# Retention in a hybrid decoder step: the output formed transposed with the values as weights, and the eight chunk states formed by one scan

## The chip, the core and the metric

The kernel is one launch on one of the eight cores of a Trainium2 chip. A core has five engines with separate instruction queues: TensorE (PE in the profile, its weight loads as PEld), VectorE (DVE), ScalarE (ACT), GpSimd (POOL) and SyncE (SP), which here issues most DMAs. Each engine runs its own queue in order; semaphores tie the queues together. TensorE reads SBUF and writes PSUM. The metric is the device time in microseconds of the launch, the median of several runs.

## The reference

The reference is one step of a decoder layer with two parallel branches, sparse attention and multi-scale retention, on a prompt of 1024 tokens and on 8 sequences of 4 new tokens. The change touches only the retention of the prompt, cut here to what is computed. There are 8 heads of 64 channels, and the prompt runs as 8 chunks of 128 tokens:

```python
def retention_chunk(state, q, k, v):
    ...
    scores = jnp.einsum('bihd,bjhd->bhij', q, k) * dmat
    out = jnp.einsum('bhij,bjhe->bihe', scores, v)
    q_decay = jnp.exp(lg[None, :] * (i[:, None] + 1.0))
    out = out + jnp.einsum('bihd,bhde->bihe', q, state) * q_decay[None, :, :, None]
    k_decay = jnp.exp(lg[None, :] * (C - 1.0 - i)[:, None])
    new_state = (jnp.exp(lg * C)[None, :, None, None] * state
                 + jnp.einsum('bjhd,bjhe->bhde', k * k_decay[None, :, :, None], v))
    return new_state, out
```

So each chunk's output is a product inside the chunk (scores times values) plus the queries times the state left by the chunks before it, and the state is a recurrence over the chunks: old state times one constant per head, plus this chunk's keys times values. The last state is an output of the layer. After it come a norm over each head's 64 channels, a gain and a gate.

## The kernel before

The program is written as one long Python function and its instructions are put into each engine's order by a scheduler that works with its own estimate of time; inside a group made by `together` the order is fixed. The chip then runs each engine's queue strictly in that order.

The stages, with the times of the profiled run: loads and norm (to about 90 us), a long stretch of projections of the input (to about 820 us) into which other work is woven, the prompt's attention (to 1030 us), and the output projection. A projection (`project`, L356 to L367) computes 128 output columns: three pieces of 352 tokens, each of 24 matrix products (L208, L209, L210: 8 steps of high and low parts), into one of two PSUM buffers `pj`. A buffer is free for the piece after next when ACT, and for some projections DVE as well, has read it. The weights of the next projection are loaded by SP (L188), and split by ACT (L194) and DVE or POOL (L195).

Two things are woven into the projections from about 160 us to 560 us:

- Retention, one `pair` of heads at a time (L428 to L567), four pairs one after the other. Each pair projects keys, queries, values and a gate (L458 to L479), turns keys and values into token rows (`kd`, `vtok`), and then does the retention. After a pair follow the projection of attention queries (`split_rows`, whose pieces are read by L391 on ACT and L392 on DVE, and the last by L396 too) and two of gates (L573).
- The selection of the top 256 keys for each query (`pick_all`, L793 to L807): 31 rounds of a bisection, in each of which DVE counts five blocks (L727), ACT counts two (L734), and DVE joins them into the next candidate (L743, L741, L803, L805). It ends with `finish` (L771 to L783), a fixed sequence of DVE operations on the seven blocks. DVE is nearly full while this runs.

The retention of a pair, where the change lies, has these steps:

- L484: for each of the 8 chunks and both heads, keys times values, into the PSUM tile `pk` (chunk by chunk, 64 columns each). The two heads of a pair occupy partitions 0 to 63 and 64 to 127.
- L486 to L488: a copy of chunk 0 and seven dependent DVE operations form the eight states `S`, chunk after chunk. The last one goes out by DMA (L489).
- L495 to L500: scores of keys and queries in two halves of four chunks, each multiplied by the decay mask on DVE into a tile `tmp` (`sT`).
- L507: queries times state, for chunks 7 to 1 and both heads. The stationary operand is the queries' 64 x 128 block of one head, the moving one the 64 columns of `S`. Result: tokens on partitions.
- L510: scores times values, stationary the 128 x 128 score block, moving the 64 columns of values, added to the same PSUM tile `po`.
- L512: ACT copies `po` into `O`, tokens on partitions.
- L516 to L539: the same for the 8 sample sequences: L524 and L529 to L532 on TensorE, L535 forms their state update `pn`, L538 adds it on DVE.
- L544 to L567: the norm over `O`, which begins on DVE with L544, then transposes (L563) back to channels on partitions, gain and gate, and a DMA out.

PSUM in this stage holds two buffers each of `pj`, `pl` (two banks) and `pt` (one bank); `pk`, `pn` and the transposes take turns in `pt`.

Of the kernel before, what the change touches and what calls it, by code (L numbers as in the profile page):

```python
# [8 lines left out]
F32 = mybir.dt.float32  # L9
# [4 lines left out]
OP = mybir.AluOpType  # L14
# [32 lines left out]
C_HM = C_SB8 + 16  # L47
C_ALL = C_HM + 32

R_G, R_GS, R_MB, R_ALL = 0, 4, 8, 16  # L50

M_D, M_S, M_ALL = 0, 256, 320


def shape_constants():
    f = np.float32
    p = np.arange(128)
    c = np.zeros((128, C_ALL), f)
    c[:, C_ID:C_ID + 128] = np.eye(128, dtype=f)
    c[:, C_CAUS:C_CAUS + 128] = np.where(p[None, :] > p[:, None], f(BIGNEG), f(0))  # L60
    b = np.arange(8)
    t = np.arange(32)
    c[:, C_MSK:C_MSK + 256] = (t[None, :] // 4 == b[:, None]).astype(f).reshape(1, 256)
    c[:, C_SEL:C_SEL + 32] = (p[:, None] % 32 == t[None, :]).astype(f)
    c[:32, C_MN:C_MN + 32] = np.where((t[None, :] // 4 == t[:, None] // 4) & (t[None, :] % 4 <= t[:, None] % 4),
                                      f(0), f(BIGNEG))
    c[0, C_BSEL:C_BSEL + 128] = 1.0
    for i in range(32):
        c[1 + i // 4, C_BSEL + 128 + i] = 1.0
    c[:, C_MH:C_MH + 8] = ((p[:, None] // 4) % 8 == b[None, :]).astype(f)  # L70
    c[:, C_SB8:C_SB8 + 16] = ((p[:, None] // 32 == t[None, :16] // 4) & (p[:, None] % 4 == t[None, :16] % 4)).astype(f)
    for q in range(4):
        c[:, C_HM + 8 * q:C_HM + 8 * q + 8] = (p[:, None] // 64 + 2 * q == b[None, :]).astype(f)
    r = np.zeros((128, R_ALL), f)
    m = np.zeros((4, 128, M_ALL), f)

    rot = np.zeros((4, 2, 128, 2 * TT), f)
    inv = (f(10000.0) ** (-np.arange(32, dtype=f) / f(32))).astype(f)
    pos = np.concatenate([np.arange(T), PAST + np.arange(NS) % NI]).astype(f)
    ang = (pos[:, None] * inv[None, :]).astype(f).T  # L80
    cos, sin = np.tile(np.cos(ang), (2, 1)), np.concatenate([-np.sin(ang), np.sin(ang)])
    step = np.concatenate([np.arange(T) % 128, np.arange(NS) % NI]).astype(f)
    size = np.concatenate([np.full(T, 128), np.full(NS, NI)]).astype(f)
    lg = np.log1p(-np.exp2(-5.0 - np.arange(8, dtype=f))).astype(f)
    df = (p[None, :] - p[:, None]).astype(f)
    ds = (t[None, :] - t[:, None]).astype(f)
    ok = (t[None, :] // 4 == t[:, None] // 4) & (ds >= 0)
    for h in range(8):
        q, i = divmod(h, 2)
        rows = slice(64 * i, 64 * i + 64)  # L90
        m[q, :, M_D + 128 * i:M_D + 128 * i + 128] = np.where(df >= 0, np.exp(lg[h] * f(-128.0)), 0)
        m[q, :32, M_S + 32 * i:M_S + 32 * i + 32] = np.where(ok, np.exp(lg[h] * f(-4.0)), 0)
        for a, decay in enumerate((np.exp(lg[h] * (size - f(1.0) - step)) * f(0.125), np.exp(lg[h] * (step + f(1.0))))):
            rot[q, a, rows, :TT] = cos * decay[None, :]
            rot[q, a, rows, TT:] = sin * decay[None, :]
        r[rows, R_G + q] = np.exp(lg[h] * f(128.0))
        r[rows, R_GS + q] = np.exp(lg[h] * f(4.0))
    r[:32, R_MB:R_MB + 8] = (t[:, None] // 4 == b[None, :]).astype(f)
    return c, r, m, rot
# [20 lines left out]
def _hybrid_step(ctx, tc, A, outs, dbg):  # L120
    nc = tc.nc
# [17 lines left out]
    def pl():  # L139
        return ps.tile([128, 1024], F32, name="pl", bufs=2)  # L140

    def pt():
        return ps.tile([128, 512], F32, name="pt", bufs=2)
# [3 lines left out]
    ident = C[:, C_ID:C_ID + 128]  # L147
# [83 lines left out]
    with ExitStack() as s0:  # L231
# [8 lines left out]
        rows = sp.tile([48, 128], F32, name="rows")  # L240
# [144 lines left out]
    def split_rows(pool, f0, p, dst, new, x=None):  # L385

        hl = [pool.tile([128, TT], F32R, name="raw", bufs=2) for _ in "hl"]

        def use(c, y):
            sl = slice(c * CH, c * CH + CH)  # L390
            nc.scalar.copy(hl[0][:, sl], y)  # L391
            nc.vector.tensor_sub(hl[1][:, sl], y, f32(hl[0][:, sl]))  # L392
            if x is not None:
                nc.scalar.copy(x[:, sl], y)  # L394
            if c == 2:
                nc.scalar.copy(new[:, p], y[:, CH - NS:])  # L396
        project(f0, use)
        for d, t in zip(dst, hl):
            nc.sync.dma_start(d[128 * p:128 * p + 128], f32(t[:, :T]))
# [3 lines left out]
    def retention(gp):  # L403
        with ExitStack() as s3:
            rp = s3.enter_context(tc.tile_pool(name="rp", bufs=1, reuse_waits="tile"))
            RC = rp.tile([128, R_ALL], F32, name="rc")
            nc.sync.dma_start(RC, A["rcs"])
            O = rp.tile([128, 9, 2, 64], F32, name="O")
            nc.gpsimd.memset(O[:, 8], 0.0)
            for p in range(4):  # L410
                pair(rp, RC, O, p)
                split_rows(gp, O_QA + 128 * p, p, QD, qs)
                gates(gp, (4 + 2 * p, 5 + 2 * p))

    def big(rp, name):
        return rp.tile([128, 9, 128], F32, name=name, bufs=2 if name == "tmp" else 1)
# [8 lines left out]
                nc.tensor.transpose(p[:n, t - 4 * g], src[:, t * 128:t * 128 + n], ident)  # L425
            use(4 * g, m, 128 if g < 2 else NS, p)

    def pair(rp, RC, O, p):  # L428
        flat = lambda t: t.rearrange("p t c -> p (t c)")[:, :TT]
        head = [slice(64 * i, 64 * i + 64) for i in (0, 1)]  # L430
        DM = rp.tile([128, M_ALL], F32, name="dm")
# [27 lines left out]
        qT = rotated(O_QR + 128 * p, "qrT", 1)  # L459
        vtok = rp.tile([128, 9, 128], F32, name="vtok")  # L460
        kd = rp.tile([128, 9, 128], F32, name="kd")
# [11 lines left out]
        def use_z(c, ps_):  # L473
# [5 lines left out]
        project(O_ZR + 128 * p, use_z)  # L479


        S = rp.tile([128, 8, 64], F32, name="S")
        pk = pt().rearrange("p (c e) -> p c e", e=64)
        together([lambda c=c, i=i: nc.tensor.matmul(pk[head[i], c], kd[:, c, head[i]], vtok[:, c, head[i]], start=True, stop=True)  # L484
                  for c in range(8) for i in (0, 1)])
        nc.vector.tensor_copy(S[:, 0], pk[:, 0])  # L486
        for c in range(1, 8):
            nc.vector.scalar_tensor_tensor(S[:, c], S[:, c - 1], RC[:, R_G + p:R_G + p + 1], pk[:, c], op0=OP.mult, op1=OP.add)  # L488
        nc.sync.dma_start(st_out[0, 0, 2 * p:2 * p + 2].rearrange("h d e -> (h d) e"), S[:, 7])  # L489


        sT = []
        for g in (0, 1):
# [5 lines left out]
            t = flat(big(rp, "tmp"))[:, :1024].rearrange("p (i c x) -> p i c x", i=2, c=4)  # L499
# [3 lines left out]
            sT.append(t)  # L503


        po = pl().rearrange("p (i c e) -> p i c e", i=2, c=8)
        together([lambda c=c, i=i: nc.tensor.matmul(po[:, i, c], qT[head[i], 128 * c:128 * c + 128], S[head[i], c - 1], start=(c == 7), stop=False)  # L507
                  for c in range(7, 0, -1) for i in (0, 1)])
        for g in (0, 1):
            together([lambda c=c, i=i: nc.tensor.matmul(po[:, i, c], sT[g][:, i, c % 4], vtok[:, c, head[i]], start=False, stop=(c == 7))  # L510
                      for c in range(4 * g, 4 * g + 4) for i in (0, 1)])
        nc.scalar.copy(O[:, :8].rearrange("p c i e -> p i c e"), po)  # L512


        qm = rp.tile([128, NB, NS], F32, name="qm")
# [42 lines left out]
        for g in range(3):  # L558
            p_ = pt()
            m = 4 if g < 2 else 1  # L560
# [9 lines left out]
    def gates(gp, js):  # L570
        for j in js:
            t = gp.tile([128, TT], F32, name="raw", bufs=2)
            project(O_GA + 128 * j, lambda c, x: nc.scalar.activation(t[:, c * CH:c * CH + CH], x, AF.Tanh, scale=0.5))  # L573
            nc.sync.dma_start(TG[128 * j:128 * j + 128], t)
# [4 lines left out]
    k_out, v_out, ki_out, st_out, ks_out, vs_out, kis_out, sts_out = outs[2:]  # L579

    with ExitStack() as s1:
# [4 lines left out]
        with ExitStack() as s2:  # L586
# [35 lines left out]
            for g in range(3):  # L622
                p = pt().rearrange("p (t c) -> p t c", c=128)
# [47 lines left out]
            for G in (0, 1):  # L671
                p = pt()[:, :128]
                nc.tensor.matmul(p, SX[:NS, 128 * G:128 * G + 128], dw.rearrange("p h t -> p (h t)"), start=True, stop=True)
                t = ip.tile([128, 4, NS], F32, name="wt", bufs=2)
# [4 lines left out]
            for G in (0, 1):  # L679
                KP = []  # L680
                for b in range(4 * G, 4 * G + 4):
# [5 lines left out]
                    p = pt()  # L687
# [5 lines left out]
                x, xn = pl(), pt()  # L693
                for o in (0, 64):
                    for b4 in range(4):
                        nc.tensor.matmul(x[32 * b4:32 * b4 + 32, 8 * o:8 * o + 512], QF[o:o + 64, 4 * G + b4], KP[b4][o:o + 64],
                                         start=True, stop=True)
# [8 lines left out]
            x, xn = pl(), pt()  # L706
# [282 lines left out]
    for p in range(4):  # L989
        x = tl.tile([128, TT], F32, name="kx", bufs=1)  # L990
        split_rows(tl, O_KA + 128 * p, p, KD, ks, x)
        token_rows(tl, x, p, k_out, ks_out, None)
    for p in range(4):
        x = tl.tile([128, TT], F32, name="raw", bufs=2)
# [109 lines left out]
    with ExitStack() as s4:  # L1104
# [18 lines left out]
        for p in range(4):  # L1123
            for group in ((7, 0, 6, 1), (5, 2, 4, 3)):
                po = [None]
# [153 lines left out]
```

## Time and profile before

| what | value |
|---|---|
| median of 3 runs | 1189.28 us (1185.84 to 1189.39) |
| the profiled execution's own time | 1189.59 us |
| its span, first to last instruction | 1187.8 us |
| mean granted TensorE clock | 0.972 of full |
| TensorE busy | 1108.8 us (93%) |
| VectorE busy | 664.8 us (56%) |
| ScalarE busy | 454.3 us (38%) |
| GpSimd busy | 329.7 us (28%) |

The busy time of TensorE counts each product from its start to its modelled end, and products overlap; what a group costs in the queue is read from the start of one group to the start of the next. A product of two f32 operands appears as two records. A row of a timeline gives start, length, engine, line, operation, the tiles (out from in), how many instructions follow each other with equal names, and in brackets the idle time before it with what ended it. A row of waits gives who waited for whom, with the total in us, the number of times and the longest.

### The profile page before, as it was taken

How to read it: one execution, taken by the hardware profiler on the slowest of the kernel's cores; microseconds unless marked ns; L12 is line 12 of the kernel's file. 1: busy time of each engine (PE TensorE's matmuls, PEld its weight loads, DVE VectorE, ACT ScalarE, POOL GpSimd, SP SyncE). 2: the span in 40 equal slices, each digit the busy share in tenths (PEclk: the TensorE clock that was granted, in tenths of full speed). 3: DMA queues.
4: the chain of work that ended last, by engine and by line, in shares of the span. 5: the costliest groups of instructions: out<-in, count | busy, mean ns of one | idle time of the engine just before them, and what ended most of it. 6: DMA issues, size and time to landing. Idle time of an engine off the chain costs nothing. (4 is left out here: it accounts for less than half of the span.)

```text
span 1187.8 us, 20303 instructions
## 1 busy us (share of the span) xinstructions
PE 1108.8 (93%) x8040; PEld 1011.9 (85%) x8040; DVE 664.8 (56%) x1599; ACT 454.3 (38%) x874; POOL 329.7 (28%) x258
## 2 busy tenths in 40 slices
PE   4999999999989959999998999999997999988997
PEld 3899989999889959999998999777976888886786
DVE  6765359999999996023222122100364766586655
ACT  5365455554555202122233332211343656432211
POOL 3413016024212511241321212242132333484000
PEclk9899999999999978999999999999998999999999
DMA  9913244144224323332775776687898551586221
GB/s 308 244 35 105 73 122 129 26 151 119 74 78 127 110 57 113 93 106 65 265 252 177 223 215 185 198 287 245 243 246 230 156 159 46 161 248 186 96 104 54
DMA packets 157892, 181.51 MB, mean 153 GB/s; under 512 B 18837, under 2 KB 129501, under 8 KB 156710
## 3 DMA queue, kind: packets, MB, share of 16 engines
q1 hardware_dynamic: 147864, 144.51, 41.5%
q0 software_dynamic: 9856, 35.66, 9.2%
q8 instruction: 63, 1.03, 0.4%
q14 instruction: 31, 0.25, 0.1%
q10 hardware_dynamic: 78, 0.06, 0.0%
HBM read 137.81 MB, written 38.60 MB: 149 GB/s over the span
## 5 line engine op out<-in xcount | busy, mean ns | idle before, releaser
L208 PE MATMUL pj<-hh,wh 128*128 128x352 f32 x1176 | 387.9, 330 | 8.7 <-ACT kx L394 3.7
L210 PE MATMUL pj<-hh,wl 128*128 128x352 f32 x1176 | 382.8, 325 | 0.0
L209 PE MATMUL pj<-hl,wh 128*128 128x352 f32 x1176 | 382.7, 325 | 0.0
L208 PEld LDWEIGHTS pj<-hh,wh 128*128 128x128 f32 x1176 | 223.0, 190 | 18.5 <-issue 6.4
L210 PEld LDWEIGHTS pj<-hh,wl 128*128 128x128 f32 x1176 | 223.2, 190 | 3.9 <-issue 3.4
L209 PEld LDWEIGHTS pj<-hl,wh 128*128 128x128 f32 x1176 | 223.6, 190 | 3.3 <-issue 2.5
L727 DVE TENSOR_SCALAR_CACHE_REDUCE eq<-sc,cand 128x896 bf16<-128x896 f32 (+4 forms) x155 | 135.7, 876 | 2.3
L195 POOL TENSOR_TENSOR wl<-ws,wh 128x1024 fp32r<-128x1024 f32 (+1 forms) x33 | 65.1, 1973 | 187.7 <-ACT wh L194 187.7
L194 ACT CAST wh<-ws 128x1024 fp32r<-128x1024 f32 (+1 forms) x65 | 61.2, 942 | 102.8 <-PE pj L209 66.3
L195 DVE TENSOR_TENSOR wl<-ws,wh 128x1024 fp32r<-128x1024 f32 x32 | 40.0, 1250 | 87.1 <-ACT wh L194 81.2
L1064 POOL TENSOR_SCALAR lg<-lg,st 128x1024 f32<-128x1024 f32 (+7 forms) x64 | 47.4, 746 | 93.4 <-DVE st L1063 83.9
L1062 ACT ACTIVATE lg<-lg,st 128x1024 f32<-128x1024 f32 (+7 forms) x64 | 49.5, 774 | 34.4 <-DVE st L1061 34.1
L734 ACT ACTIVATE ra<-sc,cand 128x1024 bf16<-128x1024 f32 x31 | 35.7, 1151 | 65.1 <-DVE cand L805 65.1
L910 POOL DMA_INDIRECT kv<-in_cache_k,idx x32 | 30.9, 965 | 102.8 <-PE str L940 84.7
L942 DVE COPY kt<-str 128x512 f32<-128x512 f32 x32 | 22.1, 690 | 61.0 <-PE str L940 53.8
L910 POOL DMA_INDIRECT kv<-in_cache_v,idx x32 | 31.7, 992 | 72.4 <-PE sx L968 43.3
L1215 PE MATMUL pj<-woh,MH 128*128 128x512 f32 (+1 forms) x136 | 51.5, 380 | 0.0
L1217 PE MATMUL pj<-woh,ML 128*128 128x512 f32 (+1 forms) x136 | 51.2, 377 | 0.0
L1216 PE MATMUL pj<-wol,MH 128*128 128x512 f32 (+1 forms) x136 | 51.2, 377 | 0.0
L573 ACT ACTIVATE raw<-pj 128x352 f32<-128x352 f32 x48 | 22.1, 460 | 72.5 <-PE pj L210 65.6
L1077 PE MATMUL tr<-C,lg 128*128 128x128 f32 x288 | 43.6, 275 | 0.8 <-DVE pT L1079 0.3
L1057 DVE CUSTOM_DVE_ANT_0 lg<-lg,bi 128x512 f32<-128x512 f32 (+3 forms) x64 | 37.1, 587 | 9.0 <-PE lg L1056 8.4
(337 smaller groups left out, 2054.4 us busy)
## 6 DMA issues: line engine op xcount, KB each, us to landing
ws<-in_w_in SPq DMA_DIRECT2D x51, 512.0 KB
TG<-raw SPq DMA_DIRECT2D x16, 528.0 KB
rot<-in_rot SPq DMA_DIRECT2D x8, 1056.0 KB
wa<-in_w_ada SPq DMA_DIRECT2D x16, 512.0 KB
u<-TG SPq DMA_DIRECT2D x8, 528.0 KB
RT<-u SPq DMA_DIRECT2D x8, 528.0 KB
t<-TG SPq DMA_DIRECT2D x8, 528.0 KB
u<-RT SPq DMA_DIRECT2D x8, 528.0 KB
```

Of the source, the lines that this page charges most:

```text
L194: nc.scalar.copy(wh[:, :, :n], ws[:, :, :n])
L195: (nc.vector if len(order) % 3 else nc.gpsimd).tensor_sub(wl[:, :, :n], ws[:, :, :n], f32(wh[:, :, :n]))
L208: nc.tensor.matmul(p, wh[:, k], HH[k][:, sl], start=(k == 0), stop=False)
L209: nc.tensor.matmul(p, wh[:, k], HL[k][:, sl], start=False, stop=False)
L210: nc.tensor.matmul(p, wl[:, k], HH[k][:, sl], start=False, stop=(k == KT - 1))
L727: nc.vector.tensor_scalar(junk[:n, :W], sc, thr[:n, j:j + 1], 0.0, op0=op, op1=OP.add, accum_out=cnt[:n, j:j + 1])
L910: nc.gpsimd.indirect_dma_start(out=t.rearrange("p s c -> p (s c)"), out_offset=None, in_=cache.rearrange("g (r s) h d -> (g r) (s h d)", s ...
L1062: nc.scalar.activation(l, l, AF.Exp, bias=st[:, 2:3], scale=0.125, accum_out=st[:, 3:4])
L1064: nc.gpsimd.tensor_scalar(l, l, st[:, 0:1], 0.5, op0=OP.mult, op1=OP.mult)
L1215: nc.tensor.matmul(x, MH[:, k, tk], wh[:, k], start=(k == 0), stop=False)
L1216: nc.tensor.matmul(x, MH[:, k, tk], wl[:, k], start=False, stop=False)
L1217: nc.tensor.matmul(x, ML[:, k, tk], wh[:, k], start=False, stop=(k == KT - 1))
```

## The change

Three things are exchanged inside `pair`; everything behind `O` stays.

The state recurrence becomes one scan. L484 writes its results with the chunk as the fastest index (stride 8), so that along the free dimension the eight chunks of one state element stand next to each other; one `tensor_tensor_scan` over 512 elements multiplies by a constant row and adds. The constant row `M_G` is the head's decay, with a zero wherever a new element begins; it is part of the mask table loaded for each pair, which grows from 320 to 832 columns.

The states are placed on the diagonal of `SD`, a new tile of 8 blocks of 128 x 128 that is set to zero once and whose off-diagonal quarters stay zero. Two ACT copies per pair do that, one for each head, and the last state goes out from there with two DMAs instead of one.

The output is formed transposed. For queries times state the stationary operand is the 128 x 128 block of `SD`, the moving one the 128 tokens of both heads' queries: seven products instead of fourteen. For scores times values the stationary operand is the 64 columns of values, the moving one the 128 x 128 scores. The result has channels on partitions, so ACT copies it to SBUF in two halves, TensorE turns it back with eight transposes, and ACT copies the halves into `O`.

```diff
-R_G, R_GS, R_MB, R_ALL = 0, 4, 8, 16
-
-M_D, M_S, M_ALL = 0, 256, 320
+R_GS, R_MB, R_ALL = 0, 4, 12
+
+M_D, M_S, M_G, M_ALL = 0, 256, 320, 832
...
+        m[q, rows, M_G:M_G + 512] = np.where(np.arange(512)[None, :] % 8 > 0, np.exp(lg[h] * f(128.0)), 0)
...
+            SD = rp.tile([128, 8, 128], F32, name="SD")
+            nc.gpsimd.memset(SD, 0.0)
             for p in range(4):
-                pair(rp, RC, O, p)
+                pair(rp, RC, O, SD, p)
...
-        S = rp.tile([128, 8, 64], F32, name="S")
-        pk = pt().rearrange("p (c e) -> p c e", e=64)
-        together([lambda c=c, i=i: nc.tensor.matmul(pk[head[i], c], kd[:, c, head[i]], vtok[:, c, head[i]], start=True, stop=True)
+        S = rp.tile([128, 512], F32, name="S")
+        pk = pt()
+        by_chunk = pk.rearrange("p (e c) -> p c e", c=8)
+        together([lambda c=c, i=i: nc.tensor.matmul(by_chunk[head[i], c], kd[:, c, head[i]], vtok[:, c, head[i]], start=True, stop=True)
                   for c in range(8) for i in (0, 1)])
-        nc.vector.tensor_copy(S[:, 0], pk[:, 0])
-        for c in range(1, 8):
-            nc.vector.scalar_tensor_tensor(S[:, c], S[:, c - 1], RC[:, R_G + p:R_G + p + 1], pk[:, c], op0=OP.mult, op1=OP.add)
-        nc.sync.dma_start(st_out[0, 0, 2 * p:2 * p + 2].rearrange("h d e -> (h d) e"), S[:, 7])
+        nc.vector.tensor_tensor_scan(S, DM[:, M_G:M_G + 512], pk, 0.0, op0=OP.mult, op1=OP.add)
+        for i in (0, 1):
+            nc.scalar.copy(SD[head[i], :, head[i]], S[head[i]].rearrange("p (e c) -> p c e", c=8))
+            nc.sync.dma_start(st_out[0, 0, 2 * p + i], SD[head[i], 7, head[i]])
...
-        po = pl().rearrange("p (i c e) -> p i c e", i=2, c=8)
-        together([lambda c=c, i=i: nc.tensor.matmul(po[:, i, c], qT[head[i], 128 * c:128 * c + 128], S[head[i], c - 1], start=(c == 7), stop=False)
-                  for c in range(7, 0, -1) for i in (0, 1)])
+        po = pl()
+        together([lambda c=c: nc.tensor.matmul(po[:, 128 * c:128 * c + 128], SD[:, c - 1], qT[:, 128 * c:128 * c + 128],
+                                               start=(c % 4 == 3), stop=False) for c in range(7, 0, -1)])
         for g in (0, 1):
-            together([lambda c=c, i=i: nc.tensor.matmul(po[:, i, c], sT[g][:, i, c % 4], vtok[:, c, head[i]], start=False, stop=(c == 7))
+            together([lambda c=c, i=i: nc.tensor.matmul(po[head[i], 128 * c:128 * c + 128], vtok[:, c, head[i]], sT[g][:, i, c % 4],
+                                                        start=False, stop=(c % 4 == 3))
                       for c in range(4 * g, 4 * g + 4) for i in (0, 1)])
-        nc.scalar.copy(O[:, :8].rearrange("p c i e -> p i c e"), po)
+        oT = flat(big(rp, "tmp"))[:, :1024]
+        for g in (0, 1):
+            half = slice(512 * g, 512 * g + 512)
+            nc.scalar.copy(oT[:, half], po[:, half])
+            x = pt()
+            for j in range(4):
+                c0 = 512 * g + 128 * j
+                nc.tensor.transpose(x[:, 128 * j:128 * j + 128], oT[:, c0:c0 + 128], ident)
+            nc.scalar.copy(O[:, 4 * g:4 * g + 4].rearrange("p t i e -> p (t i e)"), x)
```

The scheduler also orders the neighbourhood anew. The engines' built orders of the two programs differ only in the stretch of the four pairs. Between the scores (L495) and queries times state, the four pairs have 48, 48, 46 and 26 projection products before the change and 31, 26, 28 and 16 after it. L535 (the samples' state update), which stood right behind L495, stands behind the new transposes and L532.

More of the change, by code (lines that the diff above doesn't have):

```diff
@@ L95, in shape_constants @@
             rot[q, a, rows, TT:] = sin * decay[None, :]
-        r[rows, R_G + q] = np.exp(lg[h] * f(128.0))
         r[rows, R_GS + q] = np.exp(lg[h] * f(4.0))
@@ L426, in to_tokens, with pair @@
             use(4 * g, m, 128 if g < 2 else NS, p)
-    def pair(rp, RC, O, p):
+    def pair(rp, RC, O, SD, p):
         flat = lambda t: t.rearrange("p t c -> p (t c)")[:, :TT]
```

## The prediction

> **What bounds the kernel now.** I read the slices of the span first, then who waited for whom on TensorE while the four pairs run, then the timelines around the longest wait.
>
> ```profile
> DVE  6765359999999996023222122100364766586655
> PEclk9899999999999978999999999999998999999999
> ```
>
> Each digit is 1/40 of the span, 29.7 us. Counted from 0, VectorE is full in slices 6 to 14 (178 to 445 us), where the key selection runs beside the pairs. While the pairs run TensorE's clock falls visibly once, in slices 14 and 15 (416 to 475 us).
>
> ```profile
> PE pl L507 <- DVE S L488: 12.2, 1, 12.2
> ```
>
> That is the longest wait of TensorE between 100 and 570 us: queries times state waits for the chain of states on VectorE, once. The timeline of TensorE shows it in the third pair:
>
> ```profile
> 417.89 1.07 PE L535 MATMUL pt<-vm,kd 32*64 32x512 f32 x4
> 418.90 0.43 PE L208 MATMUL pj<-hh,wh 128*128 128x352 f32 x1
> ...
> 426.16 0.32 PE L208 MATMUL pj<-hh,wh 128*128 128x352 f32 x1
> 438.66 3.25 PE L507 MATMUL pl<-S,qrT 64*128 64x64 f32 x28 [12.18 <-DVE S L488]
> 441.84 7.09 PE L510 MATMUL pl<-vtok,tmp 128*128 128x64 f32 x32
> 448.86 0.32 PE L524 MATMUL pl<-qrT,krT 64*32 64x32 f32 x4
> ...
> 453.38 0.32 PE L208 MATMUL pj<-hh,wh 128*128 128x352 f32 x1
> ```
>
> Between 418.90 and 426.16 stand 45 steps of the projection, 0.161 us each. Then TensorE is idle, and afterwards slow: in the first pair the same two groups took 1.78 and 3.79 us:
>
> ```profile
> 224.07 1.78 PE L507 MATMUL pl<-S,qrT 64*128 64x64 f32 x28
> 225.78 3.79 PE L510 MATMUL pl<-vtok,tmp 128*128 128x64 f32 x32
> 229.49 0.25 PE L524 MATMUL pl<-qrT,krT 64*32 64x32 f32 x4
> ```
>
> A shorter pause in the second pair shows the price of one slow projection step, (340.65 - 337.43) / 11 = 0.293 us:
>
> ```profile
> 335.45 1.08 PE L529 MATMUL pl<-st,qm 64*32 64x64 f32 x32 [1.97 <-ACT O L512]
> ...
> 337.43 0.49 PE L208 MATMUL pj<-hh,wh 128*128 128x352 f32 x1
> ...
> 340.65 0.37 PE L210 MATMUL pj<-hh,wl 128*128 128x352 f32 x1
> ```
>
> So the third pair loses 12.2 us of idle time and, by the slow clock, 1.5 + 3.3 us in the two groups and, between the end of L524's group (448.86 + 0.32) and 453.38, 4.2 x (1 - 0.161 / 0.293) = 1.9 us in projections: 6.7 us.
>
> VectorE's timeline tells why. It is at the end of the selection, and the chain's seven steps stand between long operations of it, the last step at 439.55:
>
> ```profile
> 417.52 2.61 DVE L478 SCALAR_TENSOR_TENSOR zsT<-zt,zsT 128x352 f32<-128x352 f32 x1
> ...
> 423.29 0.69 DVE L783 TENSOR_SCALAR bis<-ra 32x1056 bf16<-32x1056 f32 x1
> ...
> 436.26 1.23 DVE L780 TENSOR_TENSOR_SCAN ra<-eq 128x512 f32<-128x512 f32 x1
> ...
> 439.55 0.28 DVE L488 SCALAR_TENSOR_TENSOR S<-S,rc,pt 128x64 f32<-128x64 f32 x1
> 439.74 0.53 DVE L392 TENSOR_TENSOR raw<-pj,raw 128x352 fp32r<-128x352 f32 x1
> ...
> 446.73 1.02 DVE L781 SCALAR_TENSOR_TENSOR ra<-ra,rem,eq 128x768 f32<-128x768 f32 x1
> ```
>
> Until then VectorE sets TensorE's time: what TensorE gains or loses in the first two pairs is swallowed by this wait.
>
> **The change part by part, TensorE first.** Prices come from these rows, the last two from the groups by form:
>
> ```profile
> 914.06 2.12 PE po L1094 x36
> ...
> 473.43 1.04 PE L563 MATMUL pt<-C,O 128*128 128x128 f32 x8
> 474.22 0.40 PE L210 MATMUL pj<-hh,wl 128*128 128x352 f32 x1
> ```
>
> ```profile
> L702 ACT ACTIVATE rl<-pl 128x512 f32<-128x512 f32 x4 | 4.2, 1176 | 3.6 <-PE pl L696 3.6
> L464 ACT COPY vtok<-pt 128x512 f32<-128x512 f32 x8 | 4.7, 589 | 0.0
> ```
>
> Removed per pair: L507 and L510, 229.49 - 224.07 = 5.42 us. Added: scores times values with 64 columns as weights and 128 moving, which is the shape of L1094: 32 records at 2.12 / 36 = 59 ns, 1.88 us, instead of 3.71. Queries times state in 14 records of full 128 x 128 blocks; the nearest row is L510 (116 ns a record, its block is as large) and the upper end twice L1094's record (118): 1.62 to 1.65 us. Eight transposes as L563: 0.79 us. Together 4.3 us, a gain of 1.1 a pair, which counts only in the fourth; in the third it is inside the walk below.
>
> L484 now writes with a stride of 8. No TensorE row shows such a write; free, or, by the ratio of the strided ACT row to the plain one (1176 / 589 = 2), 1.1 us a pair (it takes 32 records of 34 ns now):
>
> ```profile
> 414.83 1.15 PE L484 MATMUL pt<-vtok,kd 128*64 128x64 f32 x32
> 415.91 2.05 PE L495 MATMUL pl<-qrT,krT 64*128 64x128 f32 x30
> ```
>
> I take half, so the fourth pair is worth 0.5 us. The Trainium skill speaks against this edit: "SBUF — State Buffer", section "Door 1: The DMA port swizzle", says that PSUM is organised in lines of 8 bytes and that any non-contiguous PSUM pattern significantly slows matmuls. It gives no factor; no run here shows such a write yet.
>
> **VectorE and ACT.** Off VectorE go a copy and seven steps, about 0.19 us of its queue each (439.55 to 439.74), 1.5 us a pair; on it comes a scan of 512, 1.23 us by L780. That saves 0.3 a pair. ACT gets two copies into the diagonal (read with stride 8) at 0.59 to 1.18 us; nearest is L702, strided by 8 on its output: 1.18. It gets four half copies at 0.59 instead of one whole. The mask table grows by 256 KB a pair, the one memset of POOL comes before the first pair, a second state DMA is issued on SP: all have tens of us before their first reader, so I cost them at nothing; without that cover it would be some us of SP's queue, on which the next weights wait.
>
> **The third pair, walked through.** In the built order the scan stands where 423.29 stands now, with one more piece of L478 ahead of it (0.5) and 0.3 saved in each of two pairs: 423.2 us. Bounds: 2.1 earlier if L478's long hold goes (417.52: 2.61 where it takes 0.5 at other times, while POOL ran the next row), 2.4 later if two pairs' new ACT copies each delay a round of the selection by 1.2, two copies.
>
> ```profile
> 415.37 4.37 POOL L195 TENSOR_TENSOR wl<-ws,wh 128x1024 fp32r<-128x1024 f32 x1 [6.07 <-ACT wh L194]
> ```
>
> Then scan 1.23, two copies 2.36: TensorE goes on at 426.8, not 438.66. It arrives 28 products after 417.9 (L535 has moved), at 422.4 or a little earlier: a wait of 4 to 8 us replaces 12.2, and the clock falls again.
>
> What is late next is the projection's buffers. Its third piece is freed by L392 and L396, and in the built order that L392 stands far back on VectorE. From the scan to it stands all that now lies from 423.29 to 446.73 (23.4 us), without the chain (1.5) and one L478 (0.5), with the scan (1.2), one more L392 (0.5), L526 (64 columns, under 0.3 by L488) and four operations at the prices of these rows, 0.75 + 1.34 + 1.23 + 0.17:
>
> ```profile
> 455.74 0.75 DVE L538 SCALAR_TENSOR_TENSOR st<-st,rc,pt 128x512 f32<-128x512 f32 x1 [0.18 <-PE pl L529]
> 456.40 1.34 DVE L544 TENSOR_REDUCE mu<-O 128x18 f32<-128x1152 f32 x1
> 457.98 1.23 DVE L195 TENSOR_TENSOR wl<-ws,wh 128x1024 fp32r<-128x1024 f32 x1 [0.23 <-ACT wh L194]
> 459.12 0.17 DVE L545 TENSOR_SCALAR mu<-mu 128x18 f32<-128x18 f32 x1
> 459.20 0.52 DVE L392 TENSOR_TENSOR raw<-pj,raw 128x352 fp32r<-128x352 f32 x1
> ```
>
> That is 26.9 us: L392 starts at 450.1 and the buffer is free at 450.8 (0.52 + 0.19).
>
> ```profile
> 459.75 0.19 ACT L396 COPY qs<-pj 128x32 f32<-128x32 f32 x1 [1.46 <-DVE raw L392]
> ...
> 464.71 0.47 ACT L573 ACTIVATE raw<-pj 128x352 f32<-128x352 f32 x1 [1.80 <-PE pj L210]
> ```
>
> The piece that uses it ended at 464.7 and so began 24 x 0.161 earlier, at 460.8. Would TensorE be there? It took 460.8 - 438.7 = 22.1 us from L507; now 6.7 less if the clock stays up, 18 products (2.9), L535 (1.0) and the transposes (0.8) more, 1.9 less for the two groups: 18.2, so 445.0, or 450.4 if both groups run at half speed (1.6 + 1.9) and the projections lose 1.9 as now. Either way VectorE's release at 450.8 decides, and the gain there is 460.8 - 450.8 = 10.0 us. If TensorE waits there, its clock falls once more (12 steps x 0.13 = 1.6 us); I take 0.8.
>
> Behind that the built orders are the same, TensorE is near full, and the later waits follow its own progress. **Sum**, against the profiled execution's 1189.6 us (1187.8 span): 10.0 - 0.8 + 0.5 = 9.7 gained, 1179.9; that execution lies 0.3 above the median: 1179.6. With the scan's bounds and 1 us for the rest the likeliest case's own range is 1176.5 to 1183.
>
> On the clock the skill ("TensorE: Matmul & The Clock Gate", section "HAM oscillation") asks for no idle gap over about 3.4 us. The row at 335.45 does not agree: 1.97 us of idle were followed by slow steps. By the rule a short wait at 450.8 would cost nothing, and the sum would be 1178.8.
>
> **Rivals.** (1) The second release is not late, since VectorE is earlier or TensorE, slow, arrives after it: then TensorE goes on from 426.8 by itself and is there at 445.0 to 449, a gain of 12 to 16: about 1175. For it: the two arrivals are close. Against: VectorE's list is long.
>
> (2) A wait takes the place of the one removed: L544 and L538 now wait for the new transposes and for L535, which was long done. Both engines' orders then hold each other: TensorE late by x moves the release by x. VectorE is at L544 about 8.5 us before that L392 (the operations of the four rows, 3.5, and five of 768 columns near the 1.02 of L781), near 441.6; TensorE is done with L535 47 products (7.6) before the end of the walk, at 437.4 to 442.8. With 8 us more of delay in TensorE (copies on ACT held up, a slow strided product) the time is about 1187.5.
>
> (3) Slower: the selection itself is held up in pairs one and two. ACT runs in order, and counts of the selection stand behind each of the three new groups of copies, which wait for the scan, the products and the transposes. A round takes 331.69 - 325.95 = 5.7 us and ACT's spare time in it is 51.6 / 21 = 2.5:
>
> ```profile
> 325.95 0.17 DVE L805 TENSOR_SCALAR cand<-base 128x7 int32<-128x7 int32 x1
> ...
> 331.69 0.17 DVE L805 TENSOR_SCALAR cand<-base 128x7 int32<-128x7 int32 x1
> ```
>
> ```profile
> ACT ra L734 <- DVE cand L805: 51.6, 21, 5.8
> ```
>
> If each of the six groups costs the selection half a round, 2.9 us, the scan comes 17 us later and the time is 1197. It decides once the six together cost VectorE more than the gain, 1.6 us each. Against: by the walk the products end before ACT is free.
>
> (4) The change does not do what it says, the strided product being as slow as the skill warns: to eat the gain in the fourth pair alone, 32 records must take 10.8 us instead of 1.1; then 1189.
>
> **How the numbers follow.** Likeliest 0.57, (1) 0.12, (2) 0.13, (3) 0.15, (4) 0.03. Predicted is the likeliest, 1179.6. A measurement of this kernel tells 0.3% (3.6 us) from no change. Faster: the first two, 0.69; same: (2) and (4), 0.16; slower 0.15. The range goes from 1171, below (1), to 1191, above (2) and (4), and leaves (3) out.
>
> **What would show it.** On TensorE in the third pair: a wait of 4 to 8 us at the state product, ended by the diagonal copies; 14 records in 1.6 us and 32 in 1.9 where the clock is up, eight transposes in 0.8; a second wait around 450 ended by L396 or L392; the third piece after it beginning 10 us earlier. On VectorE a scan of 1.2 us near 423; on ACT diagonal copies of 0.6 to 1.2. Wrong would be: the scan starting after 427 (rival 3, seen as waits of L743 for ACT), no second wait (rival 1), VectorE idle before L544 or L538 (rival 2), or L484's group well over 2.2 us (rival 4).

## The result and the profile after

| | before | after |
|---|---|---|
| median | 1189.0 us (4 runs, 1185.84 to 1189.39) | 1177.18 us (4 runs, 1175.07 to 1179.02) |
| profiled execution's time, its span | 1189.59, 1187.8 | 1177.1, 1175.0 |
| mean granted clock | 0.972 | 0.981 |

The ratio is 0.991 (95% interval 0.988 to 0.993), so the change makes the kernel about 1% faster. The forecast was 1179.6. In the lines below a number of the source is some lines higher than before: L484 is now L488, L507 is L511, L510 is L514, L392 is L393, L396 is L397; L544 is L557, L538 is L551; L490 is the scan, L492 the diagonal copies, L524 the new transposes. The experiments' kernels have line numbers of their own, a few lines off; the tiles tell what a row is.

The slices of the span (two rows of the page):

```profile
DVE  6865349999999996123223222102256767576655
PEclk9999999999999988999999999999998999989999
```

VectorE is full in the same slices as before, 6 to 14. The clock still falls in slices 14 and 15, to 8 instead of 7 and 8. The waits of TensorE from 190 to 580 us (total, times, longest):

```profile
PE pl L511 <- ACT SD L492: 8.7, 2, 7.5
PE pj L209 <- ACT qs L397: 5.8, 2, 5.0
```

The one wait of 12.2 us has become two, at the state product for the diagonal copies, and at a projection buffer. TensorE's timeline in the third pair shows both:

```profile
408.45 1.15 PE L488 MATMUL pt<-vtok,kd 128*64 128x64 f32 x32
409.53 2.05 PE L499 MATMUL pl<-qrT,krT 64*128 64x128 f32 x30
...
415.90 0.32 PE L209 MATMUL pj<-hh,wh 128*128 128x352 f32 x1
423.71 3.36 PE L511 MATMUL pl<-qrT,SD 128*128 128x128 f32 x14 [7.49 <-ACT SD L492]
427.00 2.10 PE L514 MATMUL pl<-tmp,vtok 128*64 128x128 f32 x32
429.03 0.25 PE L537 MATMUL pl<-qrT,krT 64*32 64x32 f32 x4
...
432.98 1.09 PE L524 MATMUL pt<-C,tmp 128*128 128x128 f32 x8
434.00 1.08 PE L542 MATMUL pl<-st,qm 64*32 64x64 f32 x30
...
443.87 0.32 PE L211 MATMUL pj<-hh,wl 128*128 128x352 f32 x1
449.15 0.66 PE L209 MATMUL pj<-hh,wh 128*128 128x352 f32 x1 [4.96 <-ACT qs L397]
...
454.59 0.34 PE L209 MATMUL pj<-hh,wh 128*128 128x352 f32 x1
```

What to see: the strided product L488 takes 409.53 - 408.45 = 1.08 us, as L484 did (415.91 - 414.83). L511 is slow after its wait (3.3 us), but L514 already runs close to full speed (2.0 us, 1.9 where the clock is up); before, both groups and 4.2 us of projections were slow. From 449.15 to 454.59 stand 18 projection steps of 0.30 us, 2.5 us more than 18 x 0.161. The piece that starts at 449.15 began before the change at 460.70, without a wait, because TensorE itself was late:

```profile
460.70 0.32 PE L208 MATMUL pj<-hh,wh 128*128 128x352 f32 x1
```

VectorE and ACT, each in its own timeline:

```profile
413.68 0.15 DVE L787 TENSOR_SCALAR rem<-cnt 128x7 f32<-128x7 f32 x1
...
420.15 1.20 DVE L490 TENSOR_TENSOR_SCAN S<-dm,pt 128x512 f32<-128x512 f32 x1
...
448.36 0.52 DVE L393 TENSOR_TENSOR raw<-pj,raw 128x352 fp32r<-128x352 f32 x1
```

```profile
421.39 2.27 ACT L492 COPY SD<-S 64x512 f32<-64x512 f32 x2 [11.16 <-DVE S L490]
...
448.91 0.19 ACT L397 COPY qs<-pj 128x32 f32<-128x32 f32 x1 [3.00 <-DVE raw L393]
```

The selection's last sweep begins (rem) within 0.7 us of before, but the state is there long before:

```profile
414.38 0.15 DVE L774 TENSOR_SCALAR rem<-cnt 128x7 f32<-128x7 f32 x1
...
430.10 0.22 DVE L486 COPY S<-pt 128x64 f32<-128x64 f32 x1
```

The chain began at 430.10, behind the sweep's block of 1024 columns, and ended at 439.83. The scan stands ahead of that block, all but its first operation (L792, 0.73 us).

### The profile page after: what moved, and what is told of

Same layout as the page of the kernel before. It is cut to its first block, busy times and chain, and to the rows that moved or that the text cites. A ratio compares the mean times of both kernels' runs of the same rounds, so it can differ in the third digit from the quotient of the medians.

```text
span 1175.0 us, 20273 instructions
## 1 busy us (share of the span) xinstructions
PE 1099.4 (94%) x8016; PEld 1001.4 (85%) x8016; DVE 660.2 (56%) x1571; ACT 466.5 (40%) x894; POOL 331.6 (28%) x259
```

## The experiments

Eleven kernels ran. Ratios are to the kernel before as it ran beside them (its medians there: 1189.4 us for e1 to e4, 1190.36 for e5 to e8, 1190.75 for e9 to e11).

| run | what | median us | ratio, 95% interval |
|---|---|---|---|
| e1 | before, chain in one piece | 1191.34 | 1.002 (1.000 to 1.003) |
| e2 | state part alone | 1196.18 | 1.004 (1.003 to 1.006) |
| e3 | output part alone | 1168.73 | 0.983 (0.979 to 0.987) |
| e4 | after, buffer freed earlier | 1171.32 | 0.986 (0.982 to 0.990) |
| e5 | before, chain where the scan stands | 1188.18 | 0.999 (0.996 to 1.002) |
| e6 | before, sweep held back | 1173.64 | 0.987 (0.983 to 0.991) |
| e7 | after, sweep held back | 1168.67 | 0.983 (0.978 to 0.987) |
| e8 | output part alone, sweep held back | 1165.71 | 0.980 (0.976 to 0.985) |
| e9 | after, scan later | 1171.41 | 0.984 (0.980 to 0.988) |
| e10 | after without the diagonal | 1176.59 | 0.988 (0.984 to 0.992) |
| e11 | e8 without the diagonal | 1168.46 | 0.980 (0.976 to 0.984) |

Several of them move the selection's last sweep. It goes through seven blocks: the samples' (6), then 1024, 384, 512, 640, 768 and 896 columns (5, 4, 3, 2, 1, 0). A block can be held behind an instruction of the retention, which the code keeps in `marks`:

```diff
             for j, (sc, bi, n, W) in reversed(list(enumerate(VB + AB))):
+                with ExitStack() as hold:
+                    if j in HOLD:
+                        hold.enter_context(tc.issue_after(marks[HOLD[j]]))
```

The scheduler makes the rest of the order anew, and that turned out to matter. The number of projection products between keys times values and the state product, in the four pairs of the built orders:

| before | after | e2 | e3 | e5 | e6 | e7 | e8 | e9 |
|---|---|---|---|---|---|---|---|---|
| 48, 48, 46, 26 | 31, 26, 28, 16 | 25, 18, 19, 13 | 78, 72, 96, 42 | 48, 48, 23, 26 | 48, 48, 23, 26 | 31, 26, 16, 16 | 78, 72, 40, 42 | 31, 26, 78, 16 |

e4 and e10 have the counts of the changed kernel, e1 has 48, 48, 26, 26 and e11 48, 59, 30, 32.

### e1: the chain in one piece

```diff
+    HOLD = {4: ('chain', 2), 2: ('raw', O_QA + 256, 1), 0: ('raw', O_QA + 256, 2)}
```

A mark names an instruction: the last step of the chain of pair 2 (pairs counted from 0, so the third), and the second and the third piece of the attention-query projection that follows the third pair (`raw`, counted from 0).

> The kernel before with its chain of eight small VectorE steps and its output products unchanged; only the place in VectorE's queue differs: the selection's last blocks stand behind the third pair's chain and behind the second and third piece of the query projection's L392. My theory (the gain is the place of the state update in VectorE's queue, not cheaper work): the third pair's state product starts at 425 to 429 instead of 438.7, no wait over 3 us is left at it or at the projection's buffers, time 1174 (1171 to 1180). Rival A (the gain is TensorE's cheaper output products and the scan, which this kernel lacks): 1187 to 1190. Rival B (the second release is fixed by VectorE's amount of work, wherever the chain stands): the buffer comes free at 450 again, 1179 to 1182.

The time was 1191.3 us, far from the 1174 expected. The state product started at 435.84, with a wait of 11.9 us. I had put the chain in one piece but behind the block of 1024 columns, where it already was; closing its gaps gains nothing. The hold had also brought the samples' operations forward on VectorE, which then idled for TensorE:

```profile
446.40 0.21 DVE L528 TENSOR_TENSOR ss<-pl,dm 32x64 f32<-32x64 f32 x1 [3.50 <-PE pl L526]
453.07 0.75 DVE L540 SCALAR_TENSOR_TENSOR st<-st,rc,pt 128x512 f32<-128x512 f32 x1 [6.45 <-PE pl L531]
...
462.60 0.52 DVE L394 TENSOR_TENSOR raw<-pj,raw 128x352 fp32r<-128x352 f32 x1
```

The third piece's buffer came free after 462.6 instead of 459.2. As a test of the place the run failed; e5 repeats it.

### e2 and e3: each half alone

e2 keeps the state part and forms the output as before, from `SD[head[i], c - 1, head[i]]`. e3 keeps the chain, copies its states to the diagonal, and has the transposed output.

```diff
 e2
...
+        po = pl().rearrange("p (i c e) -> p i c e", i=2, c=8)
+        together([lambda c=c, i=i: nc.tensor.matmul(po[:, i, c], qT[head[i], 128 * c:128 * c + 128], SD[head[i], c - 1, head[i]], start=(c == 7), stop=False)
...
 e3
...
-        nc.vector.tensor_tensor_scan(S, DM[:, M_G:M_G + 512], pk, 0.0, op0=OP.mult, op1=OP.add)
+        for c in range(1, 8):
+            nc.vector.scalar_tensor_tensor(S[:, c], S[:, c - 1], RC[:, R_G + p:R_G + p + 1], pk[:, c], op0=OP.mult, op1=OP.add)
...
         for i in (0, 1):
...
+            nc.scalar.copy(SD[head[i], :, head[i]], S[head[i]])
```

> The changed kernel's state part alone: strided state product, scan and diagonal copies, but queries times state and scores times values with tokens on partitions as before, without the transposes. My theory: most of the gain stays, since the scan is one entry of VectorE's queue near 423: TensorE goes on at 426 to 429, 1178 to 1182. Rival A (the cheaper output products carry the gain): 1185 to 1188. Rival C (the diagonal copies on ACT eat it): TensorE goes on after 432, 1184 or more.

> The changed kernel's output part alone: the chain of eight VectorE steps as before, copied to the diagonal by ACT, then the transposed output. My theory: the chain is again spread between long selection steps, so the third pair's state product starts at 435 to 439, and what is gained is the order behind it and the fourth pair's 1 us: 1186 (1183 to 1189). Rival A (TensorE's savings count in all pairs, 1.1 us each, and in what follows): 1177 to 1182.

Both came out on the other side: e2 slower than the kernel before (1196.2 us), e3 faster than the whole change (1168.7). Timelines of VectorE and TensorE of e2:

```profile
432.38 1.22 DVE L490 TENSOR_TENSOR_SCAN S<-dm,pt 128x512 f32<-128x512 f32 x1
...
452.39 0.52 DVE L393 TENSOR_TENSOR raw<-pj,raw 128x352 fp32r<-128x352 f32 x1
```

```profile
435.89 3.30 PE L511 MATMUL pl<-SD,qrT 64*128 64x64 f32 x28 [11.73 <-ACT SD L492]
439.12 7.09 PE L514 MATMUL pl<-vtok,tmp 128*128 128x64 f32 x32
```

Here the scheduler left the scan behind the block of 1024 columns (432.4) and put only 19 products before the state product, so TensorE came early and waited 11.7 us; the first L393 came at 452.4, where before it was at 439.7. The early place of the scan is thus no property of the scan: it came with the whole change's order.

And of e3, TensorE's timeline:

```profile
429.73 0.66 PE L210 MATMUL pj<-hh,wh 128*128 128x352 f32 x1 [6.72 <-DVE raw L394]
...
439.49 1.72 PE L513 MATMUL pl<-qrT,SD 128*128 128x128 f32 x14
441.15 1.97 PE L516 MATMUL pl<-tmp,vtok 128*64 128x128 f32 x32
```

Its state product starts later than the one before the change (439.49 against 438.66), as I had expected, and costs no wait at all: 96 products stand ahead of it. In the third pair TensorE only waits once, 6.7 us, for a projection buffer.

### e4: the second wait taken away

```diff
+    HOLD = {1: ('raw', O_QA + 256, 2)}
```

> The changed kernel, with the selection's 768 and 896 blocks put behind the third pair's third L393, so that the projection buffer comes free at about 444 instead of 449. My theory (that release is what decides): the wait of 5.0 us and the 2.4 us of slow clock behind it go, 1170 (1168 to 1173). Rival D (something else is as late, TensorE's gain is given back at a later wait): 1175 to 1178.

As expected (1171.3 us): the buffer's wait shrinks to 1.7 us, the first one stays (its waits of TensorE):

```profile
PE pl L513 <- ACT SD L494: 8.4, 2, 7.2
...
PE pj L209 <- ACT qs L399: 2.5, 2, 1.7
```

It is 5.9 us below the changed kernel, and the two intervals (0.982 to 0.990 and 0.988 to 0.993) only just overlap. The changed kernel's second wait is set by VectorE's list, and nothing else is as late.

### e5: the old chain at the scan's place

```diff
+    HOLD = {5: ('chain', 2), 4: ('raw', O_QA + 256, 0), 2: ('raw', O_QA + 256, 1), 0: ('raw', O_QA + 256, 2)}
```

> The kernel before with its chain and its output products unchanged; only VectorE's order is the changed kernel's: the third pair's chain stands ahead of the selection's 1024 block, where the changed kernel has its scan, and the three L392 of the query projection behind the 1024 block, the 512 block and the 640 block. My theory (the place in VectorE's queue is what gains): chain done at 427 to 429, state product there instead of at 438.7, 1178 (1174 to 1183). Rival A (the cheaper transposed output carries the gain): 1186 to 1190.

The state product starts at 429.35, 9.3 us earlier than before, but the time is the same, 1188.2 us, as rival A had it. TensorE's timeline:

```profile
429.35 3.25 PE L509 MATMUL pl<-S,qrT 64*128 64x64 f32 x28 [6.23 <-DVE S L490]
432.53 7.09 PE L512 MATMUL pl<-vtok,tmp 128*128 128x64 f32 x32
439.55 0.32 PE L526 MATMUL pl<-qrT,krT 64*32 64x32 f32 x4
...
457.50 0.56 PE L208 MATMUL pj<-hh,wh 128*128 128x352 f32 x1 [2.35 <-ACT qs L398]
```

The scheduler answered with 23 products in place of 46, which come later instead (23 x 0.161 = 3.7 us). After a wait of 6.2 us the clock is down for as long as after 12.2: both groups take 10.2 us instead of 5.4, and the projections stay slow until 444.0. The piece behind the next buffer begins at 457.5 against 460.7. So the early state alone did not bring the gain. My theory fell in this form. The test is not clean: the hold put the rest of the sweep behind the pieces, and VectorE then idled 4.0 us for TensorE (until 439.92, for L526) and 0.9 us for ACT, which also made that buffer late.

### e6 to e8: VectorE not late at all

```diff
+    HOLD = {6: ('raw', O_QA + 256, 2)}
```

> The kernel before with all seven blocks of the selection's last sweep behind the third pair's third L392, so that VectorE is not late for the third pair at all (VectorE then idles a little and the selection ends later, with its readers far off). My theory: the wait of 12.2 us at the state product, its 6.7 us of slow clock and the late buffer go: 1168 (1164 to 1173). If the selection's end has a reader that now comes late: 1175 or more.

> The changed kernel with the same hold as the run before it in this call, so that neither has VectorE late in the third pair. The difference of the two is then the work that the change saves on TensorE, 1.1 us in each of four pairs with the strided write free. My theory: 3 to 6 us below that run, 1163 (1159 to 1168). Rival E (the change saves nothing but a better place on VectorE): within 2 us of that run. Rival C (the diagonal copies and the round over ACT cost more than the products save): above it.

> The output part alone (chain kept, diagonal copies, transposed output) with the same hold. If the scan itself brings 0.3 us a pair on VectorE and nothing on TensorE, it stands within 2 us of the changed kernel with that hold, 1163 (1159 to 1168); if strided write, scan and strided copies cost something, it is 2 to 5 us faster than that.

Now no wait in the third pair is over 2.7 us (e8's, at 468.2). Waits of TensorE of e6, then of e7:

```profile
PE pt L565 <- DVE tmp L568: 2.2, 1, 2.2
```

```profile
PE pl L513 <- ACT SD L494: 3.0, 2, 1.7
PE pt L578 <- DVE tmp L581: 2.4, 1, 2.4
```

With the sweep held back the old kernel gains 16.7 us (1190.36 to 1173.64), so most of what VectorE's lateness costs is to be had without the change. The changed kernel is 5.0 us below it under the same hold, though the two intervals overlap a little. The expectation took this difference for four pairs at 1.1 us, and the traces bear out only part of that. Behind the pairs e7 leads e6 by 2.3 us (the first transposes `str<-C,kv` start at 566.79 against 569.06). The lead becomes 5.0 us at a projection buffer near 620 us, where e6 waits 2.7 us and then has 10 slow steps, and e7 waits 1.4 us. It is 3.2 us at the end of the two profiled spans (e6's profiled execution, 1170.4 us, is its fastest). All three times lie above what was expected (1168, 1163, 1163), e6's and e7's just above their ranges. Whether e8's further 3.0 us are a cost of scan and strided copies is not settled: the intervals overlap widely.

### e9: a later scan

```diff
+                if j == 5:
+                    tc.add_manual_dep(marks["scan", 2], last.ins.name, ...)
```

> The changed kernel with one more order: the third pair's scan stands behind the selection's 1024 block on VectorE, where the kernel before has its chain. The scheduler then puts 78 projection products between the state's keys times values and its use, where the changed kernel has 28. Theory of the prediction (the scan's early place is the gain): the state product starts about 10 us later than 423.7, 1184 (1180 to 1188). New theory (what counts is how much projection work stands ready on TensorE while VectorE is late, and that the buffers' L394 come soon; an early scan with little work behind it is worse than a late one with much): TensorE waits twice for 1 to 2 us at projection buffers, hardly at the state, its clock stays up, 1168 (1165 to 1173).

The scan starts 10.9 us later, the state product 12.2 us later, and the time is shorter, 1171.4 against 1177.2. Timelines of VectorE and TensorE:

```profile
428.51 0.50 DVE L394 TENSOR_TENSOR raw<-pj,raw 128x352 fp32r<-128x352 f32 x1
431.06 1.20 DVE L491 TENSOR_TENSOR_SCAN S<-dm,pt 128x512 f32<-128x512 f32 x1
```

```profile
429.07 0.66 PE L209 MATMUL pj<-hh,wh 128*128 128x352 f32 x1 [10.47 <-DVE raw L394]
433.57 0.33 PE L209 MATMUL pj<-hh,wh 128*128 128x352 f32 x1
435.95 1.72 PE L512 MATMUL pl<-qrT,SD 128*128 128x128 f32 x14
```

The work ahead of the state product covers its lateness. The waits at buffers were not 1 to 2 us as the new theory had it: TensorE had finished the first piece sooner than I had reckoned and then waited 10.5 us for its L394. One wait of 10.5 us with 4.5 us of slow steps still cost less than two of 7.5 and 5.0 us with a slow stretch each.

### e10 and e11: no diagonal

```diff
...
+        together([lambda c=c, i=i: nc.tensor.matmul(po[head[i], 128 * c:128 * c + 128], S_[head[i], c - 1], qT[head[i], 128 * c:128 * c + 128],
+                                                    start=(c % 4 == 3), stop=False) for c in range(7, 0, -1) for i in (0, 1)])
```

(e11 has `S` for `S_`, and the hold of e6 to e8; e10 has no hold.)

> The changed kernel without the diagonal: fourteen products take each head's 64 x 64 state straight from the scan's result as weights (stride of 8 elements), and the last state is copied alone for its DMA. TensorE's work is the same (28 records of half the size instead of 14). If only the two diagonal copies of 1.2 us each go from the path: the third pair's wait falls from 7.5 to about 5 us, 1174 (1171 to 1178). If strided weights load slowly on TensorE (a rival): its group takes over 3 us where the clock is up and the time is 1180 or more.

> The transposed output with the chain kept, no diagonal (each head's state is the weights directly, contiguous), and the selection's last sweep held behind the third pair's third piece as in e6 to e8. The same work as e8 without the copies to the diagonal: TensorE's wait for them (1.1 us) goes, 1164 (1161 to 1168). If ACT's copies cost nothing because they are hidden: as e8, 1165.7.

e10 is as fast as the change (1176.6). The copies are off the path, and something else is as late: the third pair's wait at the state product is 7.7 us, not 5, and DVE L503 ends it (TensorE's row stands in the last section). VectorE's timeline:

```profile
424.59 2.32 DVE L503 TENSOR_TENSOR tmp<-pl,dm 128x1024 f32<-128x1024 f32 x2
```

`po` is the third `pl` tile of a pair and there are two buffers: it needs one that the decay product L503 has read. e11 equals e8 within the intervals (1168.5 against 1165.7, 1164 expected). Strided weights cost 0.2 us a group (28 records in 1.88 us in e10's first pair, 1.68 in e11's).

## Why the prediction was right, and where it was not

**The bound and the walk.** TensorE waits for VectorE in the third pair; e6 shows what that is worth. The wait at the state product was 7.5 us (forecast 4 to 8), ended by the diagonal copies, which took 2.27 us together (forecast 2.36 by the strided row). The scan started at 420.15, 1 us ahead of the lower bound: L478's long hold was gone (the 2.1 us that I had as a bound), and the sweep began 0.7 us sooner. TensorE arrived at 416.2, not 422.4: at L488 it was 6.4 us ahead of L484, 2.6 of which it had before any changed instruction of its own (the first pair's turned keys, before and after):

```profile
207.05 0.60 PE L425 MATMUL pt<-C,krT 128*128 128x128 f32 x4
```

```profile
204.42 0.60 PE L428 MATMUL pt<-C,krT 128*128 128x128 f32 x4
```

Part of the 2.6 us is a slow stretch that the run before has (8 projection steps from 201.43 to 204.14, 1.4 us) and the run after has not; the rest was not followed. The wait swallowed the lead, as the prediction said of all gains in the first two pairs.

**The second release.** L393 came at 448.36 (forecast 450.1), 28.2 us after the scan instead of 26.9, and the piece behind it began at 449.15 instead of 460.70: 11.6 us gained, forecast 10.0. TensorE was there at 444.2, so it was the release that decided, and e4 shows it by taking the lateness away. The clock took 2.5 us, 0.8 forecast (1.6 as a bound). That these add up to the forecast is partly luck: 11.6 - 2.5 is 9.1 and 10.0 - 0.8 is 9.2, but the earlier release and the longer slow stretch were each off by over 1.5 us and cancel.

**TensorE's prices.** Where the clock is up (e3) the state product takes 1.66 us and the values product 1.89 (forecast 1.62 to 1.65 and 1.88); the eight transposes take 1.0 us, not 0.79. The strided write is free, where I took half of the upper end. A pair saves 0.9 us on these; the fourth pair added 0.7 to the lead (from 8.9 us at 515 to 9.6 at 587; forecast 0.5). Once VectorE is not late (e7 against e6) the four pairs together give a lead of 2.3 us, less than 4 x 0.9 = 3.6; both runs also have slow stretches of some 10 steps at different places, which blur this.

**Mis-sized: "the later waits follow its own progress", ±1 us.** The lead grew from 9.6 us at 587 us to 13.3 at 651 (TensorE, before and after):

```profile
587.38 1.04 PE L940 MATMUL str<-C,kv 128*128 128x128 f32 x8
...
651.56 1.03 PE L940 MATMUL str<-C,kv 128*128 128x128 f32 x8
```

```profile
577.82 1.04 PE L953 MATMUL str<-C,kv 128*128 128x128 f32 x8
...
638.24 1.03 PE L953 MATMUL str<-C,kv 128*128 128x128 f32 x8
```

In between, one wait for a projection buffer fell from 3.7 to 1.5 us, and the 11 slow steps after it (1.6 us more than at full clock) are gone. TensorE's waits, before and after:

```profile
PE pj L208 <- ACT kx L394: 3.7, 1, 3.7
```

```profile
PE pj L209 <- ACT kx L395: 1.5, 1, 1.5
```

Ahead of it VectorE waits for a DMA that reads `raw`, 7.5 us before and 5.4 after. This wait follows the form of the output: in the five kernels that form it as before (before, e1, e2, e5, e6) TensorE waits 2.7 to 3.7 us there, in the eight with the transposed output 0.5 to 1.7. Why the DMA lets go sooner stays open. The sum is thus 11.6 - 2.5 + 0.7 + 3.7 = 13.5 by these rows (the lead is 13.3), of which 12.8 is left at the end of the span; the medians differ by 11.8.

**What the prediction did not see.** It took the gain as that of an earlier state. e5 and e9 speak against that: an early state with little work behind it gained nothing (e5, with VectorE idle besides), a late one with much work ahead of it gained more (e9). As far as these runs go, what counts is the number of ready projection products that the order puts between production and use, how soon VectorE frees the buffers these need, and what runs right after a wait. The order behind the change has fewer such products than before (28 against 46), and where the chain is kept with the new output (e3) they are 96, so it seems to be the scan that costs cover. On its own the state part loses 6.8 us (e2), and the output part on its own gains 20.7 us (e3), against 11.8 for the two together. Without the hold of the whole sweep, every kernel with the transposed output is at 1177.2 us or below and every one without it at 1188.2 or above. No run separates the output's form from the order that the scheduler builds around it, so how much of this gain is the cheaper products, how much the order and how much the clock is not shown.

**The rivals.** (1) did not come, TensorE did wait at the release. (2) neither: VectorE did L557 and L551 without a wait. (3) neither: the selection's last sweep began no later (413.68 against 414.38). (4) fell with 1.08 us. The Trainium skill ("SBUF — State Buffer", section "Door 1: The DMA port swizzle") says that a non-contiguous PSUM pattern significantly slows matmuls; the trace does not agree for this write, 32 records at a stride of 8 elements in the same 1.08 us. The Trainium skill ("TensorE: Matmul & The Clock Gate", section "HAM oscillation") asks for no idle gap over about 3.4 us: 4.96 us was followed by slow steps, as by that rule, but in e5 so was 2.35 us at 457.5; 2.25 us in e6 at 469.90 was not.

## What to carry to other kernels

Where one engine is late for another, these runs suggest looking in the built order at how much ready work the waiting engine has between producing an input and using the result, and who frees that work's buffers; making the late step itself cheaper can shrink that cover. Try each half of a change alone: here one half gave back part of what the other gained, and the whole did not show it. And hold back work without a near reader (here the selection's last sweep) before rewriting what waits for it: that alone brought the old kernel to 1173.6 us, and with the output part to 1165.7, the best measured here beside e11 and e7 within their intervals.

## What the runs showed of the hardware

In these runs the time that TensorE's clock stays down after a wait went with what ran next, and not with the wait's length. The granted clock is half of full in the slow stretches (0.50 from 430 to 440 us before the change), so the share of a stretch that is slow can be read from its mean. Where products with 64 moving columns follow (before, e1, e2, e5), both groups and some 4 us of projections are slow, 14 to 15 us in all, after waits of 12.2, 11.9, 11.7 and 6.2 us. Where the transposed products with 128 columns follow, it is 3.6 us in the changed kernel (wait 7.5; granted clock 0.66 from 423.71 to 429.03), 5.4 in e10 (wait 7.7) and 5.9 in e4 (wait 7.2). The rows of e10, then of e4:

```profile
425.83 3.27 PE L510 MATMUL pl<-qrT,S 64*64 64x128 f32 x28 [7.74 <-DVE tmp L503]
429.02 3.02 PE L513 MATMUL pl<-tmp,vtok 128*64 128x128 f32 x32
```

```profile
422.95 3.36 PE L513 MATMUL pl<-qrT,SD 128*128 128x128 f32 x14 [7.16 <-ACT SD L494]
426.23 3.24 PE L516 MATMUL pl<-tmp,vtok 128*64 128x128 f32 x32
```

Up to here e4 runs the same products as the changed kernel after nearly the same wait, so a spread of some 2 us has another cause than the products. Where projections with 352 columns follow, it is 4.3 to 5.5 us (e3 after 6.7 us of waiting, e9 after 10.5, the changed kernel after 5.0). By an estimate from these stretches the third pair loses 6.7 us to the slow clock before the change and 1.8 to 2.9 after it, so this is worth 4 to 5 us to the transposed output there, besides its cheaper products. No run isolates the column count from the rest of the product's shape. The Trainium skill ("TensorE: Matmul & The Clock Gate", section "Part 1: The HAM clock gate (the "warmup" mystery)") gives about 3.4 us of sustained work until the clock is back, whatever the number of products; the second and third case, 3.6 to 5.9 us, lie at or somewhat above it, the first with its 14 us far above.
